# RMS norms of a hybrid decoder step: squares added on VectorE instead of by column-grouped products of ones

## Chip, cores and metric

One core of a Trainium2 chip runs the whole program. The metric is the device time of one execution in microseconds (us); the number quoted is the median of three runs.

## The reference

One inference step of a two-layer decoder. Layer 0 mixes tokens by gated DeltaNet (GDN), layer 1 by Mamba-2 SSD; each mixer is followed by a SwiGLU feed forward (FFN). Every sublayer stands between two RMS norms over the 1024 features of a token, and SSD has one more over its 2048 gated features:

```python
def rms_norm(x, w, eps=NORM_EPS):
    xf = x.astype(F32)
    return xf * lax.rsqrt(jnp.mean(xf * xf, axis=-1, keepdims=True) + eps) * w.astype(F32)
...
        hn = rms_norm(x, mix_pre_norm[i])
...
        x = x + rms_norm(out, mix_post_norm[i]).astype(x.dtype)
        hn = rms_norm(x, ffn_pre_norm[i])
        f = (jax.nn.silu(hn @ ffn_w_gate[i]) * (hn @ ffn_w_up[i])) @ ffn_w_down[i]
        x = x + rms_norm(f, ffn_post_norm[i]).astype(x.dtype)
...
    y = rms_norm(y * jax.nn.silu(z), norm_w)
```

There are 544 tokens: 512 of one prompt and 8 sampled sequences of 4. Everything is float32.

## The kernel before, in words

**Layout.** Activations lie feature-major: 128 features on the partitions, tokens along the free dimension. The 544 columns are worked as two halves A and B of `H2` = 272. The residual stream has 8 such tiles per half (`KD` = 8).

**Products.** `product` (L232) multiplies a weight tile with a half. Both operands are split in two exact parts, and three matmuls per 128x128 tile (L239, L240, L241: high by high, high by low, low by high) add up in PSUM. Weights come by DMA five pieces ahead (`AHEAD`, `fetch_to`); each 128x512 piece is split by ACT (`wh`, L211) and DVE (`wl`, L212).

**Norms.** `Pre` is the norm ahead of a sublayer, `Post` the one behind it, and `Post.finish` goes on into the next `Pre`, tile by tile. For each of 8 tiles of a half ACT writes the square (L414 from PSUM in `Post`, L374 from `x` in `Pre`). The sum over the features is made on TensorE: a matmul with `ones[:, 0:32]` as weights puts the column sums of one square on 32 partitions of the PSUM tile `ss`, four squares going to four groups of 32 partitions, and the second four on top of them (L427 in `Post.add`, four at a time; L379 in `Pre.sum`). DVE copies `ss` to SBUF (L435, L384). `rsq` then makes the sums token-major: four matmuls with 68 columns of `ss` as weights and the column `sel` as the moving operand (L346; for SSD's post norm also L348). `sel` holds 1/1024 on one partition of each group. `rsqrt` runs 11 Newton steps on DVE (L318 to L329, 68x4 elements, tiles `nx`, `ny`, `nh`, `nt`, `nu`). `spread` writes a diagonal `dg` (L335, DVE), and one more product of ones puts the factor `r` of each token on every partition (L338). `Post.finish` then does, for each of 8 tiles, `fw *= r` (L444, DVE), `x += fw` (L446, DVE, every third tile on GpSimd) and the square of `x`; ahead of an FFN also the split `xh` (L308, ACT) and `xl` (L309, DVE).

**SSD's own norm.** `gate` takes each of 16 tiles `ys` of 128x544: times the SiLU gate (L1535, DVE), squared on ACT. After each second tile four products of ones (L1547) put the column sums of two tiles by two halves on four groups of `yss`; DVE adds that to `ssacc` (copy L1551 the first time, L1553 seven times).

**Order.** An estimated clock (`Flow`) mixes the steps of norms and mixers, written as generators, with the stream of products when the program is recorded. Engines then run their own queues in that order. So that a norm has other work beside it, the last tiles of a sublayer run half A first (`ab`), and the next sublayer begins with a few tiles of half A alone (`start_first`; 4 pairs in FFN, `NL`; 3 tiles in SSD, `SLEAD`). A **transition** below is the stretch from the `dg` of the post norm of A to the `dg` of the next pre norm of B. There are three behind a sublayer (GDN to FFN, FFN to SSD, SSD to FFN); the last FFN has only the post norm.

Of the kernel before, what the change touches and what calls it, by code (L numbers as in the profile page):

```python
# [13 lines left out]
P = 128  # L14
D = 1024
KD = D // P            # feature tiles of the residual stream
SEQ = 512
NB = 8                 # sampled sequences
TS = 4                 # tokens of each
T = SEQ + NB * TS      # columns of every feature-major tile  # L20
H2 = T // 2            # columns of one product's moving operand
TQ = H2 // 4
NC = SEQ // P          # chunks of the prompt
KFF = 22
NSQ = 6                # squares that wait for their sums
AHEAD = 5              # weight pieces fetched ahead
NL = 4                 # feed forward's pairs that start before the second half's norm
NZ = 2                 # gates of SSD before its first x
ZLAG = 3               # x tiles of SSD before the next gate
SLEAD = 3              # SSD's tiles that start before the second half's norm  # L30
FINE = 12              # SSD's first products, with other work between their pieces
WIDE = 4               # SSD's first products, with more banks
NH0 = 4                # states of sampled sequences loaded ahead
PACE = 5.0             # between two updates of sampled states
LIVE = 3               # heads of GDN scanned side by side
# [3 lines left out]
# columns of the constant block  # L39
# [6 lines left out]
def constants():  # L46
# [8 lines left out]
    c[::32, C_SEL] = 1.0 / D  # L55
    c[0::64, C_SEL + 1] = 1e-6 / 2048
    c[32::64, C_SEL + 2] = 1e-6 / 2048
# [28 lines left out]
def _program(nc, tc, io, es):  # L86
# [23 lines left out]
    # ---------------------------------------------------------------- order of emission  # L110
    class Flow:
        """Interleaves generators with the stream of products, on an estimated clock (us).
        A generator yields (time on the tensor engine, time until its next step can start),
        or a condition that its next step waits for."""
# [73 lines left out]
    # ---------------------------------------------------------------- constants  # L188
# [13 lines left out]
    sely = [cst[:, C_SEL + 1 + i:C_SEL + 2 + i] for i in range(2)]  # L202
# [11 lines left out]
    # ---------------------------------------------------------------- weights  # L214
    # plan: the weight tiles in the order in which the products want them
# [83 lines left out]
    def stack(tile, src, first):  # L299
        """[96, n] of halves for one product of three: hi hi lo if first, else hi lo hi."""  # L300
# [31 lines left out]
    def spread(y):  # L332
        """[TQ, 4] with a token of a half on each element -> [P, H2], on every partition."""
# [7 lines left out]
    def rsq(ss, e, extra=None):  # L341
        """(mean + e) ** -0.5, token-major."""
        ps = bank("ms")[0:TQ, 0:4]
        for j in range(4):
            q = slice(TQ * j, TQ * j + TQ)
            PE.matmul(ps[:, j:j + 1], lhsT=ss[:, q], rhs=sel, start=True, stop=extra is None)  # L346
            if extra is not None:
                PE.matmul(ps[:, j:j + 1], lhsT=extra[1][:, q], rhs=extra[0], start=False, stop=True)  # L348
# [3 lines left out]


    class Pre:
        """st.x[hf] -> st.xh[hf], st.xl[hf]. free: without the norm's factor, which goes to
        st.r[hf] for the products' results."""

        def __init__(self, hf, kind, layer, free=False):
            self.hf, self.free, self.x = hf, free, st.x[hf]
            self.w = lambda k: nrm[:, kind, layer, k:k + 1]  # L360
            self.ps = bank("ss")
# [3 lines left out]

        def step(self, k):
            self.sum(k, self.square(k))

        def square(self, k):
# [3 lines left out]
            t = sqp.tile([P, H2], F32, tag="sq", name="sq", bufs=NSQ)  # L373
            S.activation(out=t, in_=x, func=AF.Square)  # L374
            return t

        def sum(self, k, t):
            g = k % 4
            PE.matmul(self.ps[32 * g:32 * g + 32, 0:H2], lhsT=ones[:, 0:32], rhs=t,  # L379
                      start=k < 4, stop=k >= KD - 4)  # L380

        def end(self):
            ss = sqp.tile([P, H2], F32, tag="ss", name="ss", bufs=1)
            V.tensor_copy(out=ss, in_=self.ps[:, 0:H2])  # L384
            y = rsq(ss, 1e-6)
# [17 lines left out]
    class Post:  # L403
        """Evacuates the tiles of a sublayer's last product, then post norm and residual."""

        def __init__(self, kind, layer, fw, e=1e-6, extra=None):
            self.kind, self.layer, self.fw, self.e, self.extra = kind, layer, fw, e, extra
            self.sq = [[], []]
            st.ready = [False, False]

        def tile(self, m):
            def done(hf, ps):
                t = sqp.tile([P, H2], F32, tag="sq", name="sq", bufs=NSQ)
                S.activation(out=t, in_=ps, func=AF.Square)  # L414
                S.activation(out=self.fw(m, hf), in_=ps, func=AF.Copy,
                             scale=nrm[:, self.kind, self.layer, m:m + 1])
                self.sq[hf].append(t)
                if len(self.sq[hf]) == 1:
                    self.ps = getattr(self, "ps", [None, None])
                    self.ps[hf] = bank("ss")  # L420
                if len(self.sq[hf]) % 4 == 0:
                    flow.start(self.add(hf, len(self.sq[hf]) - 4), 1.0)
            return done

        def add(self, hf, k0):
            for g in range(4):
                PE.matmul(self.ps[hf][32 * g:32 * g + 32, 0:H2], lhsT=ones[:, 0:32],  # L427
                          rhs=self.sq[hf][k0 + g], start=k0 == 0, stop=k0 == KD - 4)
            if k0 == KD - 4:
                yield 0.0, 0.5  # L430
                yield from self.finish(hf)

        def finish(self, hf):
            ss = sqp.tile([P, H2], F32, tag="ss", name="ss", bufs=1)
            V.tensor_copy(out=ss, in_=self.ps[hf][:, 0:H2])  # L435
            y = rsq(ss, self.e, None if self.extra is None else (sely[hf], self.extra))
# [4 lines left out]
            ts = []  # L441
            for k in range(KD):
# [4 lines left out]
                ts.append(pre.square(k))  # L447
                yield 0.1, 0.6
                if k % 4 == 3 and ts[k] is not None:
                    for j in range(k - 3, k + 1):  # L450
                        pre.sum(j, ts[j])
            yield from pre.end()

    def ab(tiles, operand, tail):
        """Both halves of each tile; the last ones A first, so that A's norm has company."""
# [1261 lines left out]
```

## Time and profile before

| | us |
|---|---|
| median of 3 runs (1797.18 to 1797.25) | 1797.25 |
| profiled execution: span | 1795.2 |
| time outside the span (median less span) | 2.05 |
| PE busy | 1746.4 (97%) |
| DVE busy | 1122.2 (63%) |
| ACT busy | 818.3 (46%) |
| POOL busy | 105.5 (6%) |
| mean granted TensorE clock | 0.981 of full speed |

The profile is of one execution. PE is TensorE's stream of matmuls, DVE is VectorE, ACT ScalarE, POOL GpSimd. One float32 matmul instruction leaves two records, so that "x6" of `ss` is three instructions. Records of the same kind that touch are merged in a timeline, and their number stands behind the x. A start and a duration are in us from the start of the span. A square bracket at the end of a row tells how long the engine had been idle before it, and who released it.

### The profile page before, as it was taken

How to read it: one execution, taken by the hardware profiler on the slowest of the kernel's cores; microseconds unless marked ns; L12 is line 12 of the kernel's file. 1: busy time of each engine (PE TensorE's matmuls, PEld its weight loads, DVE VectorE, ACT ScalarE, POOL GpSimd, SP SyncE). 2: the span in 40 equal slices, each digit the busy share in tenths (PEclk: the TensorE clock that was granted, in tenths of full speed). 3: DMA queues.
4: the chain of work that ended last, by engine and by line, in shares of the span. 5: the costliest groups of instructions: out<-in, count | busy, mean ns of one | idle time of the engine just before them, and what ended most of it. 6: DMA issues, size and time to landing. Idle time of an engine off the chain costs nothing. (4 is left out here: it accounts for less than half of the span.)

```text
span 1795.2 us, 37598 instructions
## 1 busy us (share of the span) xinstructions
PE 1746.4 (97%) x14447; PEld 1620.1 (90%) x14447; DVE 1122.2 (63%) x2966; ACT 818.3 (46%) x1824; POOL 105.5 (6%) x335
## 2 busy tenths in 40 slices
PE   6999999999999999999989999999999999999997
PEld 4888888898899999999787899999998999999996
DVE  5886856354876655323777886878348666664335
ACT  4765554345643333234555565657346433333242
POOL 0122112000000000000101110100000000000000
PEclk7999999799999999999999999999999999999998
DMA  5332323234354432234535544432434444444344
GB/s 140 103 93 79 91 71 107 77 109 137 114 182 140 141 112 83 77 92 141 175 105 155 166 131 140 133 103 64 141 129 147 159 147 141 142 140 139 122 130 124
DMA packets 163124, 220.89 MB, mean 123 GB/s; under 512 B 53184, under 2 KB 66048, under 8 KB 162432
## 3 DMA queue, kind: packets, MB, share of 16 engines
q1 hardware_dynamic: 162944, 218.49, 39.5%
q8 instruction: 113, 1.85, 0.4%
q14 instruction: 67, 0.55, 0.1%
HBM read 197.39 MB, written 21.04 MB: 122 GB/s over the span
## 5 line engine op out<-in xcount | busy, mean ns | idle before, releaser
L239 PE MATMUL mm<-xh,wh 128*128 128x272 f32 x2560 | 754.2, 295 | 3.2 <-ACT raw L534 2.3
L241 PE MATMUL mm<-xh,wl 128*128 128x272 f32 x2560 | 749.6, 293 | 1.9 <-issue 1.9
L240 PE MATMUL mm<-xl,wh 128*128 128x272 f32 x2560 | 746.8, 292 | 0.0
L212 DVE TENSOR_TENSOR wl<-wr,wh 128x512 fp32r<-128x512 f32 (+1 forms) x556 | 376.0, 679 | 328.6 <-ACT wh L211 316.8
L211 ACT ACTIVATE wh<-wr 128x512 fp32r<-128x512 f32 (+1 forms) x556 | 345.0, 622 | 446.7 <-PE mm L240 408.2
L239 PEld LDWEIGHTS mm<-xh,wh 128*128 128x128 f32 x2560 | 485.2, 190 | 24.3 <-issue 12.9
L241 PEld LDWEIGHTS mm<-xh,wl 128*128 128x128 f32 x2560 | 484.4, 189 | 8.9 <-issue 7.5
L240 PEld LDWEIGHTS mm<-xl,wh 128*128 128x128 f32 x2560 | 485.1, 190 | 6.7 <-issue 3.7
L239 PE MATMUL mm<-gb,wh 128*128 128x272 f32 x576 | 167.6, 292 | 0.0
L241 PE MATMUL mm<-gb,wl 128*128 128x272 f32 x576 | 165.1, 289 | 0.0
L240 PE MATMUL mm<-gb,wh 128*128 128x272 f32 x576 | 164.5, 288 | 0.0
L239 PEld LDWEIGHTS mm<-gb,wh 128*128 128x128 f32 x576 | 108.4, 188 | 5.4 <-issue 3.5
L547 DVE SCALAR_TENSOR_TENSOR conv<-raw,cw,conv 128x512 f32<-128x512 f32 x144 | 106.6, 741 | 8.4 <-ACT conv L544 7.9
L241 PEld LDWEIGHTS mm<-gb,wl 128*128 128x128 f32 x576 | 107.8, 188 | 1.2 <-issue 0.9
L240 PEld LDWEIGHTS mm<-gb,wh 128*128 128x128 f32 x576 | 107.9, 188 | 0.7 <-issue 0.4
L1172 ACT ACTIVATE sg<-sg 128x272 f32<-128x272 f32 x88 | 37.7, 431 | 99.7 <-DVE sg L1171 99.5
L446 POOL TENSOR_TENSOR x<-x,fw 128x272 f32<-128x272 f32 x16 | 14.8, 923 | 1087.0 <-DVE fw L444 658.9
L239 PE MATMUL mm<-yh,wh 128*128 128x272 f32 x256 | 75.1, 294 | 0.0
L240 PE MATMUL mm<-yl,wh 128*128 128x272 f32 x256 | 74.3, 290 | 0.4 <-DVE yl L309 0.4
L241 PE MATMUL mm<-yh,wl 128*128 128x272 f32 x256 | 73.9, 291 | 0.7 <-DVE wl L212 0.7
L211 ACT ACTIVATE gb<-sg 128x272 fp32r<-128x272 f32 x72 | 31.1, 432 | 93.6 <-DVE sg L1180 93.6
L1171 DVE TENSOR_TENSOR sg<-mm,r 128x272 f32<-128x272 f32 x88 | 38.6, 440 | 53.4 <-PE mm L241 51.7
(404 smaller groups left out, 2460.0 us busy)
## 6 DMA issues: line engine op xcount, KB each, us to landing
wr<-f_d_in SPq DMA_DIRECT2D x110, 256.0 KB
wr<-f_g_in SPq DMA_DIRECT2D x104, 256.0 KB
wr<-f_u_in SPq DMA_DIRECT2D x104, 256.0 KB
wr<-g_w_in SPq DMA_DIRECT2D x64, 256.0 KB
wr<-s_w_in SPq DMA_DIRECT2D x48, 256.0 KB
wr<-s_wo_in SPq DMA_DIRECT2D x44, 256.0 KB
wr<-s_wz_in SPq DMA_DIRECT2D x36, 256.0 KB
ar<-ad SPq DMA_DIRECT2D x32, 272.0 KB
```

The source lines that it names most:

```text
L211: S.activation(out=hi, in_=src, func=AF.Copy)
L212: V.tensor_tensor(out=lo, in0=src, in1=hi.bitcast(F32), op=ALU.subtract)
L239: PE.matmul(ps, lhsT=h[:, k, :], rhs=ah(k0 + k), start=first and k == 0, stop=False)
L240: PE.matmul(ps, lhsT=h[:, k, :], rhs=al(k0 + k), start=False, stop=False)
L241: PE.matmul(ps, lhsT=lo[:, k, :], rhs=ah(k0 + k), start=False, stop=last and k == n - 1)
L446: E.tensor_tensor(out=x[:, k, :], in0=x[:, k, :], in1=f, op=ALU.add)
L547: V.scalar_tensor_tensor(out=Y[:, 0:SEQ], in0=R[:, j:j + SEQ], scalar=w[:, j:j + 1], in1=Y[:, 0:SEQ], op0=ALU.mult, op1=ALU.add)
L1171: V.tensor_tensor(out=t, in0=ps, in1=st.r[hf], op=ALU.mult)
L1172: S.activation(out=t, in_=t, func=AF.Silu)
```

## The change

A class `Squares` keeps one tile `acc` of 128x272 in SBUF for each norm and half. The first square of a half is written by ACT straight into it; each later one goes to a tile `sq`, and DVE adds it to `acc` (`add`). The add of a square is issued only when the next square is issued, the last one in `sum`. The products into `ss`, and the copies of `ss`, are gone; the four token-major products take `acc` itself as weights, and `sel` is now 1/1024 on all 128 partitions. In SSD ACT writes the first gated square into `yacc` (128x544), and DVE adds 15 more. `Post.finish` starts 1.0 us after the eighth tile on the estimated clock, where it was 1.5 us. There are five `sq` tiles instead of six. (The diff of the whole file also strips comments, which is left out here.)

```diff
-NSQ = 6                # squares that wait for their sums
+NSQ = 5
...
-    c[::32, C_SEL] = 1.0 / D
-    c[0::64, C_SEL + 1] = 1e-6 / 2048
-    c[32::64, C_SEL + 2] = 1e-6 / 2048
+    c[:, C_SEL] = 1.0 / D
+    c[:, C_SEL + 1] = 1e-6 / 2048
...
-                PE.matmul(ps[:, j:j + 1], lhsT=extra[1][:, q], rhs=extra[0], start=False, stop=True)
+                PE.matmul(ps[:, j:j + 1], lhsT=extra[:, q], rhs=sely, start=False, stop=True)
...
+    class Squares:
+        def __init__(self):
+            self.acc = sqp.tile([P, H2], F32, tag="acc", name="acc", bufs=2)
+            self.n, self.late = 0, None
+
+        def square(self, src):
+            if self.n == 0:
+                S.activation(out=self.acc, in_=src, func=AF.Square)
+            else:
+                t = sqp.tile([P, H2], F32, tag="sq", name="sq", bufs=NSQ)
+                S.activation(out=t, in_=src, func=AF.Square)
+                self.add()
+                self.late = t
+            self.n += 1
+
+        def add(self):
+            if self.late is not None:
+                V.tensor_tensor(out=self.acc, in0=self.acc, in1=self.late, op=ALU.add)
+                self.late = None
+
+        def sum(self):
+            self.add()
+            return self.acc
...
     class Pre:
...
-            t = sqp.tile([P, H2], F32, tag="sq", name="sq", bufs=NSQ)
-            S.activation(out=t, in_=x, func=AF.Square)
-            return t
-
-        def sum(self, k, t):
-            g = k % 4
-            PE.matmul(self.ps[32 * g:32 * g + 32, 0:H2], lhsT=ones[:, 0:32], rhs=t,
-                      start=k < 4, stop=k >= KD - 4)
+            self.ss.square(x)
 
         def end(self):
-            ss = sqp.tile([P, H2], F32, tag="ss", name="ss", bufs=1)
-            V.tensor_copy(out=ss, in_=self.ps[:, 0:H2])
-            y = rsq(ss, 1e-6)
+            y = rsq(self.ss.sum(), 1e-6)
...
     class Post:
...
-                if len(self.sq[hf]) % 4 == 0:
-                    flow.start(self.add(hf, len(self.sq[hf]) - 4), 1.0)
+                if self.ss[hf].n == KD:
+                    flow.start(self.finish(hf), 1.0)
...
-        def add(self, hf, k0):
-            for g in range(4):
-                PE.matmul(self.ps[hf][32 * g:32 * g + 32, 0:H2], lhsT=ones[:, 0:32],
-                          rhs=self.sq[hf][k0 + g], start=k0 == 0, stop=k0 == KD - 4)
-            if k0 == KD - 4:
-                yield 0.0, 0.5
-                yield from self.finish(hf)
...
-            ss = sqp.tile([P, H2], F32, tag="ss", name="ss", bufs=1)
-            V.tensor_copy(out=ss, in_=self.ps[hf][:, 0:H2])
-            y = rsq(ss, self.e, None if self.extra is None else (sely[hf], self.extra))
+            y = rsq(self.ss[hf].sum(), self.e, None if self.extra is None else self.extra[:, half(hf)])
...
-                ts.append(pre.square(k))
-                yield 0.1, 0.6
-                if k % 4 == 3 and ts[k] is not None:
-                    for j in range(k - 3, k + 1):
-                        pre.sum(j, ts[j])
+                pre.square(k)
+                yield 0.0, 0.6
...
             S.activation(out=t, in_=y, func=AF.Square)
-            yield 0.0, 2.0
-            sqs.append(t)
...
-            ps = dbank("yss")
-            for j, t in enumerate((a, b)):
-                for h in range(2):
-                    r = 32 * (2 * j + h)
-                    PE.matmul(ps[r:r + 32, 0:H2], lhsT=ones[:, 0:32], rhs=t[:, half(h)],
-                              start=True, stop=True)
...
-                V.tensor_tensor(out=ssacc, in0=ssacc, in1=ps[:, 0:H2], op=ALU.add)
-            yield 0.6, 0.5
+            yield 0.0, 1.0
+            V.tensor_tensor(out=yacc, in0=yacc, in1=t, op=ALU.add)
```

Counted over the program, TensorE loses 160 matmul instructions (128 into `ss`, 32 into `yss`). DVE loses 24 (16 copies of `ss`, one copy and seven adds of `ssacc`) and gains 127 (112 adds of 128x272, 15 of 128x544). ACT, GpSimd and the DMA queues keep their counts.

TensorE's order in the GDN to FFN transition, at the end of GDN's last product (operands `oh`, `ol`) and the start of the FFN's first (`xh`, `xl`). Before:

```order
L241 MATMUL mm<-oh,wl 128x272
L427 MATMUL ss<-sq,cst 32x272 x3
L379 MATMUL ss<-sq,cst 32x272
L427 MATMUL ss<-sq,cst 32x272
L379 MATMUL ss<-sq,cst 32x272
L239 MATMUL mm<-xh,wh 128x272
L240 MATMUL mm<-xl,wh 128x272
```

With the change:

```order
L240 MATMUL mm<-oh,wl 128x272
L238 MATMUL mm<-xh,wh 128x272
L239 MATMUL mm<-xl,wh 128x272
L238 MATMUL mm<-xh,wh 128x272
L239 MATMUL mm<-xl,wh 128x272
L345 MATMUL ms<-cst,acc 68x1 x4
```

The products of ones between the two sublayers are gone, and the token-major products come after two tiles of the next one.

DVE's order in the same transition, while half B goes through `Post.finish` and half A's first FFN tiles are evacuated (`sg`). Before:

```order
L1171 TENSOR_TENSOR sg<-mm,r 128x272
L444 TENSOR_TENSOR fw<-fw,r 128x272
L212 TENSOR_TENSOR wl<-wr,wh 128x512
L1174 TENSOR_TENSOR sg<-sg,r 128x272
L446 TENSOR_TENSOR x<-x,fw 128x272
L212 TENSOR_TENSOR wl<-wr,wh 128x512
L1180 TENSOR_TENSOR sg<-sg,mm 128x272
L309 SCALAR_TENSOR_TENSOR xl<-x,nrm,xh 128x272
L444 TENSOR_TENSOR fw<-fw,r 128x272
```

With the change:

```order
L1168 TENSOR_TENSOR sg<-mm,r 128x272
L444 TENSOR_TENSOR fw<-fw,r 128x272
L373 TENSOR_TENSOR acc<-acc,sq 128x272
L1171 TENSOR_TENSOR sg<-sg,r 128x272
L446 TENSOR_TENSOR x<-x,fw 128x272
L211 TENSOR_TENSOR wl<-wr,wh 128x512 x2
L308 SCALAR_TENSOR_TENSOR xl<-x,nrm,xh 128x272
L1177 TENSOR_TENSOR sg<-sg,mm 128x272
L444 TENSOR_TENSOR fw<-fw,r 128x272
L373 TENSOR_TENSOR acc<-acc,sq 128x272
```

Each tile of the norm brings one add more into the queue, in front of the evacuations and weight splits behind it.

DVE's order in the FFN to SSD transition, half B behind its post norm's `dg`. Before:

```order
L444 TENSOR_TENSOR fw<-fw,r 128x272 x2
L446 TENSOR_TENSOR x<-x,fw 128x272 x2
L444 TENSOR_TENSOR fw<-fw,r 128x272 x3
L446 TENSOR_TENSOR x<-x,fw 128x272 x2
L444 TENSOR_TENSOR fw<-fw,r 128x272 x3
L446 TENSOR_TENSOR x<-x,fw 128x272 x2
L384 COPY ss<-ss 128x272
L318 TENSOR_SCALAR nx<-ms 68x4
```

With the change:

```order
L444 TENSOR_TENSOR fw<-fw,r 128x272
L373 TENSOR_TENSOR acc<-acc,sq 128x272
L446 TENSOR_TENSOR x<-x,fw 128x272
L444 TENSOR_TENSOR fw<-fw,r 128x272 x2
L446 TENSOR_TENSOR x<-x,fw 128x272
L373 TENSOR_TENSOR acc<-acc,sq 128x272
L444 TENSOR_TENSOR fw<-fw,r 128x272
L373 TENSOR_TENSOR acc<-acc,sq 128x272
L446 TENSOR_TENSOR x<-x,fw 128x272
L373 TENSOR_TENSOR acc<-acc,sq 128x272
```

The adds stand between the `fw` and `x` of one chain, and the copy of `ss` at its end is replaced by the last of them.

## Rows read from the trace of the kernel before

**Rows 1.** The page, part 1: busy time, share of span, instructions.
```profile
PE 1746.4 (97%) x14447; PEld 1620.1 (90%) x14447; DVE 1122.2 (63%) x2966; ACT 818.3 (46%) x1824; POOL 105.5 (6%) x335
```
**Rows 2.** Waits of PE: who for whom: us in total, times, longest.
```profile
PE r L338 <- DVE dg L335: 14.8, 7, 6.8
```
**Rows 3.** Busy time by stretch away from the transitions; columns as headed.
```profile
core 0: us, PE busy (x) PEld busy (x) DVE busy (x) ACT busy (x) POOL busy (x), PEclk, DMA share, GB/s
417.00:437.00 20.00, 20.00 (x151) 16.97 (x150) 6.67 (x10) 10.22 (x22) 0.00 (x0) 1.00 0.38 120
795.00:850.00 55.00, 55.00 (x432) 51.86 (x431) 20.00 (x32) 23.05 (x45) 0.00 (x0) 1.00 0.43 127
1040.00:1240.00 200.00, 200.00 (x1664) 185.27 (x1664) 153.77 (x413) 114.55 (x244) 19.59 (x61) 1.00 0.38 119
...
1700.00:1756.00 56.00, 56.00 (x439) 52.75 (x438) 20.95 (x36) 23.14 (x45) 0.00 (x0) 1.00 0.44 129
```
**Rows 4.** Tile `ss`, sublayers' last products: records, ns min/median/max, first to last.
```profile
L427 PE MATMUL ss<-sq,cst x24: 392/405/417, 417.7 to 437.3; 128*32 128x272 f32 x24
...
L427 PE MATMUL ss<-sq,cst x24: 392/405/417, 1701.3 to 1755.3; 128*32 128x272 f32 x24
```
**Rows 5.** Timeline of PE, SSD's last product: start, duration, instruction.
```profile
1332.07 0.29 PE L241 MATMUL mm<-yh,wl 128*128 128x272 f32 x1
1332.29 0.66 PE L427 MATMUL ss<-sq,cst 128*32 128x272 f32 x6
...
1333.11 0.29 PE L240 MATMUL mm<-yl,wh 128*128 128x272 f32 x1
1333.23 0.29 PE L241 MATMUL mm<-yh,wl 128*128 128x272 f32 x1
1333.45 0.65 PE L427 MATMUL ss<-sq,cst 128*32 128x272 f32 x2
...
1334.26 0.29 PE L240 MATMUL mm<-yl,wh 128*128 128x272 f32 x1
```
**Rows 6.** Busy time by stretch, PE on tile `yss` alone, all of SSD.
```profile
960.00:1260.00 300.00, 7.83 (x64) 1.00 0.39 125
```
**Rows 7.** Busy time in the three transitions; columns as in rows 3.
```profile
442.48:496.70 54.22, 52.98 (x382) 44.52 (x381) 44.61 (x125) 32.93 (x73) 3.70 (x4) 1.00 0.36 117
854.81:901.06 46.25, 40.19 (x285) 31.98 (x284) 35.83 (x104) 25.22 (x55) 4.88 (x13) 0.96 0.59 189
1339.41:1399.70 60.29, 59.81 (x446) 51.95 (x445) 50.91 (x130) 36.23 (x78) 3.92 (x4) 1.00 0.44 142
```
**Rows 8.** Timeline of DVE, GDN to FFN.
```profile
473.26 0.43 DVE L1171 TENSOR_TENSOR sg<-mm,r 128x272 f32<-128x272 f32 x1
473.61 0.42 DVE L444 TENSOR_TENSOR fw<-fw,r 128x272 f32<-128x272 f32 x1
```
**Rows 9.** Timeline of DVE, GDN to FFN: its longest waits.
```profile
457.94 0.16 DVE L318 TENSOR_SCALAR nx<-ms 68x4 f32<-68x4 f32 x1 [2.46 <-PE ms L346]
...
489.41 0.44 DVE L384 COPY ss<-ss 128x272 f32<-128x272 f32 x1 [2.83 <-PE ss L379]
```
**Rows 10.** Timelines of POOL and of DVE, GDN to FFN, half A.
```profile
445.77 0.77 POOL L446 TENSOR_TENSOR x<-x,fw 128x272 f32<-128x272 f32 x1 [111.52 <-DVE fw L444]
...
445.83 1.02 DVE L309 SCALAR_TENSOR_TENSOR xl<-x,nrm,xh 128x272 fp32r<-128x272 f32 x1 [0.19 <-ACT xh L308]
...
447.12 0.49 DVE L309 SCALAR_TENSOR_TENSOR xl<-x,nrm,xh 128x272 fp32r<-128x272 f32 x1
```
**Rows 11.** Timeline of PE, FFN to SSD, half B.
```profile
893.04 1.33 PE L379 MATMUL ss<-sq,cst 128*32 128x272 f32 x4 [1.93 <-ACT sq L374]
...
901.64 1.25 PE L338 MATMUL r<-dg,cst 68*128 68x272 f32 x2 [2.56 <-DVE dg L335]
```
**Rows 12.** The last post norm: timeline of ACT, and chain of waits.
```profile
1780.59 0.40 ACT L414 ACTIVATE sq<-mm 128x272 f32<-128x272 f32 x1 [5.41 <-PE mm L241]
...
1780.56 1.15 PE ss L427 x8
...
1782.22 0.67 PE ms L346 x8
```

More of the change, by code (lines that the diff above doesn't have):

```diff
@@ L201, in _program @@
     sel = cst[:, C_SEL:C_SEL + 1]
-    sely = [cst[:, C_SEL + 1 + i:C_SEL + 2 + i] for i in range(2)]
+    sely = cst[:, C_SEL + 1:C_SEL + 2]
     I4 = cst[:, C_I4:C_I4 + 32]
@@ L360, in __init__ @@
             self.w = lambda k: nrm[:, kind, layer, k:k + 1]
-            self.ps = bank("ss")
+            self.ss = Squares()
             self.xh = act.tile([P, KD, H2], F32R, tag="x", name="xh")
@@ L364, in __init__ @@
             st.xh[hf], st.xl[hf] = self.xh, self.xl
-        def step(self, k):
-            self.sum(k, self.square(k))
         def square(self, k):
@@ L407, in __init__ @@
             self.kind, self.layer, self.fw, self.e, self.extra = kind, layer, fw, e, extra
-            self.sq = [[], []]
+            self.ss = [None, None]
             st.ready = [False, False]
@@ L412, in done @@
             def done(hf, ps):
-                t = sqp.tile([P, H2], F32, tag="sq", name="sq", bufs=NSQ)
-                S.activation(out=t, in_=ps, func=AF.Square)
+                if self.ss[hf] is None:
+                    self.ss[hf] = Squares()
+                self.ss[hf].square(ps)
                 S.activation(out=self.fw(m, hf), in_=ps, func=AF.Copy,
                              scale=nrm[:, self.kind, self.layer, m:m + 1])
[L417 to L420, printed above, removed]
-                if len(self.sq[hf]) % 4 == 0:
-                    flow.start(self.add(hf, len(self.sq[hf]) - 4), 1.0)
-            return done
-        def add(self, hf, k0):
-            for g in range(4):
-                PE.matmul(self.ps[hf][32 * g:32 * g + 32, 0:H2], lhsT=ones[:, 0:32],
-                          rhs=self.sq[hf][k0 + g], start=k0 == 0, stop=k0 == KD - 4)
-            if k0 == KD - 4:
-                yield 0.0, 0.5
-                yield from self.finish(hf)
+                if self.ss[hf].n == KD:
+                    flow.start(self.finish(hf), 1.0)
+            return done
         def finish(self, hf):
-            ss = sqp.tile([P, H2], F32, tag="ss", name="ss", bufs=1)
-            V.tensor_copy(out=ss, in_=self.ps[hf][:, 0:H2])
-            y = rsq(ss, self.e, None if self.extra is None else (sely[hf], self.extra))
+            y = rsq(self.ss[hf].sum(), self.e, None if self.extra is None else self.extra[:, half(hf)])
             yield 0.0, 1.0
@@ L440, in finish @@
             pre = self.pre(hf)
-            ts = []
             for k in range(KD):
@@ L469, in _program @@
         for k in range(KD):
-            pre.step(k)
+            pre.square(k)
     for pre in pres:
@@ L1261, in ssd @@
         dma(sdt, io["s_dt"].partition_broadcast(P))
-        ssacc = one.tile([P, H2], F32, name="ssacc")
+        yacc = one.tile([P, T], F32, name="yacc")
         cm = cone.tile([P, NB * 36], F32, name="cm")
@@ L1517, in x_task @@
             d.done = True
-        sz, sqs = {}, []
+        sz = {}
         def z_done(m):
@@ L1535, in gate @@
             V.tensor_tensor(out=y, in0=y, in1=t, op=ALU.mult)
-            S.activation(out=t, in_=y, func=AF.Square)
-            yield 0.0, 2.0
-            sqs.append(t)
-            if len(sqs) < 2:
-                return
-            a, b = sqs
-            sqs.clear()
-            ps = dbank("yss")
-            for j, t in enumerate((a, b)):
-                for h in range(2):
-                    r = 32 * (2 * j + h)
-                    PE.matmul(ps[r:r + 32, 0:H2], lhsT=ones[:, 0:32], rhs=t[:, half(h)],
-                              start=True, stop=True)
             if not hasattr(st, "first"):
                 st.first = True
-                V.tensor_copy(out=ssacc, in_=ps[:, 0:H2])
-            else:
-                V.tensor_tensor(out=ssacc, in0=ssacc, in1=ps[:, 0:H2], op=ALU.add)
-            yield 0.6, 0.5
+                S.activation(out=yacc, in_=y, func=AF.Square)
+                return
+            S.activation(out=t, in_=y, func=AF.Square)
+            yield 0.0, 1.0
+            V.tensor_tensor(out=yacc, in0=yacc, in1=t, op=ALU.add)
         W = io["s_w"]
@@ L1608, in ssd @@
         fw = [t544("fw") for _ in range(KD)]
-        post = Post(1, 1, lambda m, hf: fw[m][:, half(hf)], 1e-12, ssacc)
+        post = Post(1, 1, lambda m, hf: fw[m][:, half(hf)], 1e-12, yacc)
         post.pre = lambda hf: Pre(hf, 2, 1, True)
```

## The prediction

> **What bounds the kernel now.** I begin with the page's busy times. PE is busy for 97% of the span, DVE for 63% [rows 1]. A kernel like that gets faster where PE has less to do, unless another engine then paces it. So the second question goes to the stretches. In four steady stretches, in which a sublayer's last product runs, and in SSD, PE is busy all the time at the full granted clock, while DVE works 20.00 of 55 us there, or 6.67 of 20, and 153.77 of 200 in SSD [rows 3]. There PE alone sets the pace. In the three transitions PE is busy for 52.98 of 54.22 us, 40.19 of 46.25 and 59.81 of 60.29, but DVE for 44.61, 35.83 and 50.91 [rows 7]: PE is first, DVE a close second. The list of waits says what PE lacks when it lacks something: 14.8 us in seven waits for `dg`, the last step of a norm on DVE [rows 2].
>
> **The price of a visit.** A timeline shows what a product of ones costs in a stream of weight products. One product matmul follows another every 0.127 us (55.00 us over 432 records, [rows 3]). Around three `ss` instructions (six records) the start of L241 at 1332.07 and that of L240 at 1333.11 lie 1.04 us apart where two steps, 0.25, would do: the visit costs 0.79. The next visit has one instruction and costs 1.03 - 0.25 = 0.78 [rows 5]. So the price is for the interruption, not for the number of products. If it were only the length of a record, 0.39 us at the least [rows 4], a visit would be worth half of that.
>
> The Trainium skill ("TensorE: Matmul & The Clock Gate", Part 3, Measured speedup vs the span model) has a rule that speaks against this change: products in different column groups run side by side, about 4 ns apart, so that four cost hardly more than one. The trace agrees that three cost as much as one, but at twice the length of the record. By the rule alone a visit is worth some 0.40 us, an estimate, and the steady term below would be 8.8 and not 17.2 us.
>
> **The change part by part.** The sum is made against the profiled span, 1795.2 us; 2.05 us lie outside it up to the median, 1797.25, and I take them as unchanged.
>
> *Steady stretches.* The last products of the four sublayers contain 24 `ss` records each (two per instruction) [rows 4], which the timeline shows in 6, 5, 6 and 5 visits. They go: 22 x 0.78 = **17.2 us**. The adds that replace them (7 per half, 0.35 us of issue each: `sg` at 473.26 and `fw` at 473.61, [rows 8]) lie beside products, with DVE busy about 36% there [rows 3]; without that cover they would cost 56 x 0.35 = 20 us.
>
> *SSD.* PE spends 7.83 us in `yss` [rows 6], in twelve visits; some are next to state products that interrupt the stream anyway, so I take the busy time, **7.8 us**, and not 12 x 0.78 = 9.4; at the least half, 4. DVE gets 15 adds of 128x544, at twice the 272-column step 0.7 each, 10.5 us, and loses eight small ones, 2.8. With 46 of 200 us free [rows 3] that is covered.
>
> *Start and end.* At the start only the norms run; I credit **0.5 us**, between 0 and one visit, 0.78. At the end the chain goes from 1780.56 (the `ss` products) to 1782.22 (`ms`). Now the last square, which starts at 1780.59 and takes 0.40, is followed by one add of 0.43 [rows 8], so `ms` can start near 1781.5: **0.7 us** [rows 12].
>
> *Transitions.* Here PE loses 12, 6 and 11 visits, but DVE gains 17 adds and loses three copies in each: 17 x 0.35 - 3 x 0.36 = 4.9 us. In GDN to FFN DVE's work becomes 44.61 + 4.9 = 49.5 us, while PE's falls to 52.98 - 12 x 0.78 = 43.6 [rows 7]. DVE now paces. It still has to wait at the ends of the chains, 2.46 us for `ms` and 2.83 for the last squares' sum [rows 9]; with the copy's round trip gone I leave 3 us of waits, so 52.5 against 54.22: **1.7 us**. In SSD to FFN the order puts 22 product matmuls more ahead of B's factor, 2.8 us of work that stood behind it, with some 0.7 us of splits. DVE needs 50.91 + 4.9 + 0.7 + 3 = 59.5, against 60.29 + 2.8 = 63.1: **3.6 us**. FFN to SSD is a chain in which PE waits for squares (1.93) and for `dg` (2.56) [rows 11]. Its first part loses six visits, 4.7 us; in its second the adds between `fw` and `x` lengthen DVE's chain by up to 8 x 0.35 = 2.8, less the copy and half a visit. I take **1.5 us**, about midway between 4.7 - 1.8 = 2.9 and nothing. If no wait of DVE stayed, the three would give 4.7, 4.9 (46.25 less 35.83 + 4.9 + 0.6 of splits) and 6.6, together 16.2; if all of DVE's present idle time stayed, they would lose 4.9 and 4.9 and 2.8, together 12.6.
>
> *Small things.* Five `sq` tiles for six cost nothing while each add follows its square by one tile. The counts of ACT, POOL and DMA instructions stay.
>
> Sum: 17.2 + 7.8 + 0.5 + 0.7 + 1.7 + 3.6 + 1.5 = 33.0 us. The span becomes 1762.2, and the time **1764 us**.
>
> **The rivals.** *PE paces the transitions too.* If the scheduler's order lets DVE's adds slip into its idle time, the visits' full price comes back: 29 x 0.78 = 22.6 instead of 6.8, in all 48.8, so 1748; with 16.2, 1755. For it: DVE has 9.6, 10.4 and 9.4 us idle. Against it: that idle time is waiting inside the norm's chain, which the adds lengthen.
>
> *DVE's idle time stays, and more.* Each add stands in a chain of `fw`, `x`, square and add, over DVE and ACT, and DVE's queue is in order, so an add whose square is not ready holds the evacuations behind it. With all idle time kept, the gain is 26.2 - 12.6 = 13.6, so 1784; with half of that loss, 1777. DVE is also held by GpSimd: `xl` takes 1.02 us beside POOL's `x` and 0.49 without [rows 10]. Twelve such `x` stand in loops that get adds, so up to 12 x 0.53 = 6.4 us, 1770. The Trainium skill ("SBUF — State Buffer", SBUF: two separate sides) has this as a lock: a DVE operation with two SBUF inputs and a GpSimd operation that reads SBUF exclude each other. The adds have two SBUF inputs, as `xl` has, and the rows agree.
>
> *The steady stretches do not pay.* If weights, not PE, set their pace, PE would wait for `wl` instead, and only the transitions, start and end count: 1789. Against it: PE is busy 100% there, DMA 0.38 to 0.44 [rows 3].
>
> *Slower.* The adds of `Post` and of SSD are queued ahead of weight splits. If an add stood waiting for ACT's square of the tile just finished, then `wl` would come late and PE would stop once for each of 56 + 15 adds, for 0.40 + 0.43 = 0.83 us [rows 8, 12]: 59 us lost against 33 gained, 1797 + 26 = 1823. It decides from 33 / 71 = 0.46 us per add. Against it: the add of a square is issued only with the next square, a whole product of at least 24 x 0.127 = 3 us later, and weights are fetched five pieces ahead.
>
> *It doesn't do what it says.* The order shows the `ss` and `yss` products gone, so I give that nothing.
>
> **How the numbers follow.** My forecast, DVE pacing the transitions with some waits left, gets 0.53, with a range of its own from 1756 to 1771. PE pacing everything, 1746 to 1756, gets 0.22. DVE's idle time kept or its queue held, 1771 to 1784, gets 0.18, in it 0.01 for a visit worth no more than its record: 22 x 0.39 = 8.6 us less gain, 1772, against which the rows show 0.78. Steady stretches without pay get 0.04, slower 0.03. The range from 1748 to 1780 leaves out a small part of the second case (0.04), of the third (0.04) and the last two (0.07), some 0.15. A measurement here tells a difference from about 0.2%, 3.6 us. All cases but the last lie further below 1797.25 than that; a thin remainder where gains and losses meet gets 0.03 for no change, slower 0.03, faster 0.94.
>
> **What would show it.** Right: no `ss` or `yss` records, PE busy 45 to 50 us less, the steady stretches 3.9 to 4.7 us shorter each with PE still at 100%, SSD some 8 us shorter; adds of 0.43 us on DVE, whose busy time grows by about 48 us (112 x 0.43 + 15 x 0.71 less 24 x 0.44); in the two transitions to FFN DVE busy for over 90% and PE with new waits for `dg` beyond 14.8 us in all. Wrong: PE waits for `wl` in steady stretches or in SSD (the last two rivals); PE still at 98% in the transitions and the time near 1750 (the first); transitions longer than before (the second).

## The result and the profile after

The changed kernel took 1768.7 us (median of 4 runs, 1765.33 to 1778.71) beside 1797.22 us for the kernel before (4 runs, 1784.13 to 1797.25). The ratio is 0.9891, with a 95% interval of 0.9854 to 0.9927: faster, by about 1.1%. (It is not the quotient of the two medians, 0.9841: 0.9891 is 1768.7 over 1788.24, the median of the 15 runs of the kernel before that stand beside e1.) The forecast was 1764 us, a ratio of 0.9815 to 1797.25.

Executions of either kernel differ by some 13 us. Much of this lies in the GDN mixer, which the change does not touch: it took 355.3 to 368.4 us in the thirteen profiles of this study, by how long TensorE's granted clock lies at the lower of its two levels there. Its mean over the mixer was 0.94 in the kernel before (368.0 us), 0.96 in the changed one (362.9) and 0.99 in e4 (355.4). The windows of 50 us that hold such a stretch show it, first in the kernel before, then in the changed one:

```profile
100.00:150.00 50.00, 47.07 (x621) 41.51 (x620) 41.56 (x140) 30.25 (x79) 11.86 (x37) 1.00 0.31 74
300.00:350.00 50.00, 48.61 (x553) 39.75 (x553) 18.26 (x52) 16.43 (x49) 4.05 (x16) 0.76 0.27 83
```

```profile
100.00:150.00 50.00, 48.56 (x590) 41.89 (x589) 37.97 (x133) 28.04 (x71) 10.93 (x37) 0.86 0.30 79
300.00:350.00 50.00, 49.15 (x637) 41.29 (x637) 25.85 (x70) 21.25 (x62) 6.99 (x20) 1.00 0.34 98
```

PEclk (third column from the end) was 0.76 in one and 0.86 in the other, at different places. So below I compare two executions stretch by stretch and leave the GDN mixer out. The boundaries are the starts of the `dg` on DVE, of which there are 20 in each trace. The third column is a second profiled execution of the same changed kernel (experiment e5), the fourth the best kernel of the study (e1).

| stretch, us | before | changed | changed, e5 | adds in post norms and SSD only, e1 |
|---|---|---|---|---|
| start, to the second `dg` | 22.9 | 25.5 | 24.2 | 23.5 |
| GDN mixer, to the first of its own `dg` | 368.0 | 362.9 | 356.1 | 359.0 |
| GDN's last product, to post norm A | 43.3 | 39.4 | 39.4 | 39.1 |
| transition GDN to FFN | 54.2 | 56.1 | 53.0 | 54.1 |
| first FFN, to post norm A | 358.1 | 354.4 | 352.6 | 351.9 |
| transition FFN to SSD | 46.3 | 49.9 | 48.4 | 45.3 |
| SSD, mixer | 370.6 | 367.8 | 366.9 | 365.4 |
| SSD, last product, to post norm A | 67.8 | 63.4 | 63.4 | 63.4 |
| transition SSD to FFN | 60.3 | 60.9 | 62.3 | 61.3 |
| second FFN, to post norm A | 361.2 | 353.4 | 353.2 | 355.2 |
| end | 34.3 | 35.0 | 35.2 | 34.7 |
| whole span | 1795.2 | 1776.9 | 1763.0 | 1761.3 |
| span less the GDN mixer | 1427.2 | 1414.0 | 1406.9 | 1402.3 |

(The GDN mixer has four `dg` of its own ahead of its last product; the 8.3 us between them are in no row and the same in all. SSD is divided at ACT's 357th split of a weight piece, which lies in its last product, behind the last product into `yss` and ahead of the first into `ss`.) Outside the GDN mixer the change is thus worth 13 to 20 us where 33 were forecast; the kernel before was profiled once. The steady stretches give what they should. FFN to SSD and SSD to FFN lengthen where they should have shortened, and GDN to FFN does so in one execution of two.

The page's first part of the changed kernel, as [rows 1]:

```profile
PE 1697.0 (96%) x14127; PEld 1612.5 (91%) x14127; DVE 1162.0 (65%) x3069; ACT 818.0 (46%) x1824; POOL 110.2 (6%) x335
```

PE is busy 49 us less, DVE 40 us more. The steady stretches, as [rows 3], are still PE's alone, with DVE at 37 to 43% of them and 82% in SSD:

```profile
405.00:425.00 20.00, 20.00 (x161) 20.00 (x160) 8.62 (x16) 10.21 (x23) 0.00 (x0) 1.00 0.47 149
790.00:830.00 40.00, 40.00 (x317) 39.63 (x316) 14.71 (x26) 15.90 (x31) 0.00 (x0) 1.00 0.41 116
1016.00:1216.00 200.00, 200.00 (x1652) 187.43 (x1652) 163.79 (x440) 117.78 (x248) 22.76 (x67) 1.00 0.42 126
...
1690.00:1735.00 45.00, 45.00 (x360) 44.86 (x359) 18.79 (x31) 19.37 (x37) 0.00 (x0) 1.00 0.50 143
```

The transitions, as [rows 7], have changed places: DVE is now busy for 49.13 of 56.12 us, 42.43 of 49.86 and 53.68 of 60.89, and PE stands still for 8, 15 and 6 us of them (before 1, 6 and less than 1).

```profile
436.08:492.20 56.12, 48.29 (x327) 46.70 (x326) 49.13 (x138) 32.02 (x72) 3.49 (x4) 0.85 0.36 116
846.59:896.45 49.86, 34.79 (x258) 33.10 (x256) 42.43 (x120) 25.58 (x56) 4.99 (x13) 0.87 0.56 174
1327.59:1388.48 60.89, 54.82 (x424) 52.11 (x423) 53.68 (x145) 36.84 (x79) 5.58 (x4) 1.00 0.45 140
```

The list of PE's waits names the new one, beside the old of [rows 2]:

```profile
PE ms L345 <- DVE acc L373: 31.0, 6, 12.0
PE r L337 <- DVE dg L334: 13.9, 5, 6.4
PE mm L240 <- DVE wl L211: 5.1, 8, 1.3
```

The token-major products `ms` read `acc`, and wait for the last add; 14.9 of the 31.0 us, the longest wait of 12.0 among them, lie at the start, where there is nothing else to do. The waits for `wl`, 0.7 us in all before, lie in the transitions, 3.7 of the 5.1 us in SSD to FFN, but for one of 0.8 us in SSD that was there before; none is in a steady stretch. What the wait for `acc` brings with it stands in the timeline of PE in GDN to FFN and in windows of 4 us from there on:

```profile
444.19 0.29 PE L239 MATMUL mm<-xl,wh 128*128 128x272 f32 x1
449.10 1.06 PE L345 MATMUL ms<-cst,acc 128*68 128x1 f32 x8 [4.62 <-DVE acc L373]
...
450.62 0.43 PE L239 MATMUL mm<-xl,wh 128*128 128x272 f32 x1
450.85 0.43 PE L240 MATMUL mm<-xh,wl 128*128 128x272 f32 x1
```

```profile
444.00:448.00 4.00, 0.48 (x4) 0.26 (x2) 4.00 (x11) 3.64 (x11) 0.76 (x1) 0.82 0.00 0
448.00:452.00 4.00, 2.90 (x21) 2.90 (x21) 3.38 (x11) 0.84 (x2) 0.00 (x0) 0.50 0.22 66
452.00:456.00 4.00, 4.00 (x19) 4.00 (x19) 3.88 (x21) 1.26 (x2) 0.00 (x0) 0.50 0.61 178
456.00:460.00 4.00, 4.00 (x28) 3.92 (x28) 2.20 (x9) 1.89 (x4) 0.00 (x0) 0.90 0.50 154
```

The four matmuls ahead of `ms` are two pairs of `xh,wh` and `xl,wh`; the third matmul of a step, `xh,wl`, comes only behind it. Between them PE runs nothing for 4.62 us, while DVE is busy all the time. `ms` is not the only one that waits. The FFN's first `wl` stands in DVE's queue right behind the add that releases `ms`, 12.9 us behind the `dg`; in the kernel before it came 10.0 us behind it:

```profile
448.61 0.43 DVE L373 TENSOR_TENSOR acc<-acc,sq 128x272 f32<-128x272 f32 x1
448.97 0.68 DVE L211 TENSOR_TENSOR wl<-wr,wh 128x512 fp32r<-128x512 f32 x1
```

```profile
452.51 1.28 DVE L212 TENSOR_TENSOR wl<-wr,wh 128x512 fp32r<-128x512 f32 x2
```

In e4, where DVE wrote that first `wl` ahead of the norm's work, PE stopped a little further on, for the second one:

```profile
443.84 0.59 PE L243 MATMUL mm<-xh,wl 128*128 128x272 f32 x1 [5.25 <-DVE wl L214]
```

So DVE's queue holds PE here, by whichever of its results is wanted first. After the pause the granted clock is 0.50, the lower level (1.2 GHz), and product matmuls come 0.23 us apart in place of 0.126, until about 456 us.

This pause did not decide the length of the transition. The second execution, e5, has it too, 4.62 us with a clock of 0.50 behind it, and took 53.0 us from `dg` to `dg`, less than the kernel before (54.2) and than e1 (54.1). The 56.1 us of the first hold another stop, of 2.27 us at 482.73 for a `wh` whose weights came late (ACT had waited 2.97 us for the transfer); e5 has none there.

In FFN to SSD the pause is 9.56 us:

```profile
883.57 0.29 PE L240 MATMUL mm<-xh,wl 128*128 128x272 f32 x1
893.42 1.04 PE L345 MATMUL ms<-cst,acc 128*68 128x1 f32 x8 [9.56 <-DVE acc L373]
```

Here the lead tiles of half A are done, 3.5 us behind B's `dg`, where they lasted to 0.6 us ahead of it before; behind `ms` stand the factor `r` of half B and what follows it. What got longer is half B's chain on DVE, from `dg` to `dg`: 16.1 us, and 15.9 in e5, where it was 11.2 before (12.1 in e7, which leaves it as it was). It holds seven adds, and four weight splits `wl` where two stood before.

### The profile page after: what moved, and what is told of

The parts are those of the page before. It is cut to its first block, busy times and chain, and to the rows that moved or that the text cites. A ratio compares the mean times of both kernels' runs of the same rounds, so it can differ in the third digit from the quotient of the medians.

```text
span 1776.9 us, 37092 instructions
## 1 busy us (share of the span) xinstructions
PE 1697.0 (96%) x14127; PEld 1612.5 (91%) x14127; DVE 1162.0 (65%) x3069; ACT 818.0 (46%) x1824; POOL 110.2 (6%) x335
## 4 chain that ended last, share of the span: by engine, by line
PE 88%; DVE 6%; ACT 2%; DMA 2%; issue 1%; POOL 0%; SPq 0%; DVEq 0%; ACTq 0%; POOLq 0%
PE mm L238 25%; PE mm L240 25%; PE mm L239 24%; DVE acc L373 1%; PE yd L1495 1%; PE yos L1386 1%; PE yo L1500 1%; PE su L1472 1%; DVE wl L211 1%; PE mm L247 1%; DVE fw L444 1%; PE r L337 1%; PE sc L985 1%; PE ms L345 1%; PE su L573 1%
## 5 line engine op out<-in xcount | busy, mean ns | idle before, releaser
L373 DVE TENSOR_TENSOR acc<-acc,sq 128x272 f32<-128x272 f32 x112 | 50.1, 448 | 45.9 <-ACT sq L366 45.3
```

The lines of the kernel that those rows point to most:

```text
L373: V.tensor_tensor(out=self.acc, in0=self.acc, in1=self.late, op=ALU.add)
```

## The experiments

Theory A: the adds of the pre norms, 14 of the 17 in each transition, lie in the chain that DVE paces there and give away what the visits return. Rival B: not the adds but the new order costs, since `Post.finish` starts half a microsecond earlier and cuts in elsewhere. Rival C: GpSimd and VectorE hold each other up. Figures "outside the GDN mixer" are the profiled span less that stretch, as in the table; those of the changed kernel are 1414.0 and 1406.9 us.

**e1, adds in the post norms and SSD only.** The pre norms go back to products of ones, on the changed kernel:

```diff
 class Pre:
-            self.ss = Squares()
+            self.ps = bank("ss")
...
-            self.ss.square(x)
+            t = sqp.tile([P, H2], F32, tag="sq", name="sq", bufs=NSQ)
+            S.activation(out=t, in_=x, func=AF.Square)
+            return t
+        def sum(self, k, t):
+            g = k % 4
+            PE.matmul(self.ps[32 * g:32 * g + 32, 0:H2], lhsT=ones[:, 0:32], rhs=t,
+                      start=k < 4, stop=k >= KD - 4)
```

> The adds on VectorE are kept in the post norms and in SSD's gated norm; the pre norms sum their squares on TensorE again, as before the change. Compared by stretch, since the granted clock inside the GDN mixer differs from run to run. Theory A (the adds of the pre norms, 14 of the 17 in each transition, lie in the chain that VectorE paces there, and give away what the visits return): the three transitions are back near those of the kernel before, 54, 46 and 60 us (plus or minus 2), and the steady stretches and SSD keep the shortening that the changed kernel has there, 4.4, 2.7, 6.2, 3.6 and 4.8 us, so some 5 us less than the changed kernel at equal clock. Rival B (the order: the post norm's chain now starts half a microsecond earlier on the estimated clock and cuts in elsewhere; the adds themselves are free): GDN to FFN and FFN to SSD stay at 56 and 50 us or so, and the time stays within 2 us of the changed kernel's.

Measured: 1762.79 us (4 runs, 1761.88 to 1763.06) beside 1788.24 for the kernel before (15 runs), ratio 0.9853 (0.983 to 0.9876). The transitions are back:

```profile
429.92:484.03 54.11, 53.83 (x381) 45.23 (x380) 46.82 (x129) 33.66 (x76) 4.03 (x4) 1.00 0.40 124
835.94:881.24 45.30, 40.00 (x290) 33.39 (x288) 37.05 (x108) 25.80 (x56) 4.68 (x13) 0.93 0.63 197
1310.07:1371.40 61.33, 60.77 (x444) 52.59 (x443) 51.29 (x134) 36.31 (x79) 3.24 (x4) 1.00 0.45 142
```

PE is busy throughout the first and third again, and the clock is 1.00 in them. The rest of the gain stayed. Outside the GDN mixer it is 5 to 12 us under the changed kernel. `Post.finish` starts early here too, so rival B is out as the main cause. Something of it is there: in FFN to SSD half B's chain has the four weight splits here too, and takes 13.3 us (12.4 in e6) without any add, beside 11.2 before.

**e2, adds in the pre norms only.** The same edit the other way round: `Post` and SSD as before the change, `Pre` with `Squares`.

> Only the pre norms add on VectorE; the post norms and SSD sum on TensorE as before the change. Theory A: steady stretches and SSD as before (within 1 us each); the transitions are longer than before by 0 to 4 us each, the start by 1 to 2, and the whole is 3 to 10 us slower than before at equal clock although some 23 visits of 0.78 us are gone from the transitions. Rival B: the transitions are as before or up to 6 us shorter each, and the whole is faster than before.

Measured: 1794.97 us (10 runs) beside 1788.24, ratio 1.0038 (1.0019 to 1.0057): slower. Transitions 55.3, 48.6 and 62.0 us, the start 24.9; outside the GDN mixer 1430.8 beside 1427.2. The pre norms' visits are gone from PE, and nothing came of it, as A says. Half B's chain in FFN to SSD takes 13.5 us, with the adds but only two weight splits.

**e3, the pre norms' adds doubled.** In the changed kernel:

```diff
         def add(self):
             t = self.late.pop(0)
+            for _ in range(self.dose):          # 1 in Pre, 0 in Post
+                self.eng.tensor_tensor(out=t, in0=t, in1=t, op=ALU.max)
             self.eng.tensor_tensor(out=self.acc, in0=self.acc, in1=t, op=ALU.add)
```

> The changed kernel with each add of the pre norms preceded by one operation more on VectorE of the same size (the square's maximum with itself, which leaves it as it is): 42 more in the transitions, 14 at the start. Theory A (VectorE paces the transitions): each costs its 0.35 us there, so some 4 to 5 us more in each transition and 2 to 4 at the start, 14 to 19 us in all. Rival B (adds are free in the transitions, the order costs): under 4 us in all.

Measured: 1797.37 us (6 runs), ratio 1.0048 (1.0021 to 1.0075), so all of the gain is lost. The start is 28.8, the transitions 59.7, 53.4 and 66.2: against the two executions of the changed kernel 3.3 to 4.6 us longer at the start and 3.6 to 6.7, 3.5 to 5.0 and 3.9 to 5.3 in the transitions. For 14 operations each that is 0.25 to 0.5 us apiece: in a transition little hides DVE's work. Outside the GDN mixer the time is 1428.8 us, 15 to 22 more than the changed kernel's; 14 to 19 were expected.

**e4, the post norms' adds doubled.** The same line in `Post`'s `Squares`.

> The changed kernel with each add of the post norms preceded by one operation more of the same size: 56 more, most of them in the steady stretches, some 3 of each sublayer behind the first dg of a transition. Theory A: nothing in the steady stretches (under 0.5 us each), at most 1 us in each transition and 0.4 at the end, 0 to 4 us in all. If the steady adds held VectorE's queue in front of the weight splits (the slower rival of the prediction), 0.3 us or more for each, 15 us and more.

Measured: 1774.62 us (4 runs), ratio 0.992 (0.9896 to 0.9943). The steady stretches are 40.4 (from 39.4), 352.8 (352.6 to 354.4), 63.8 (63.4) and 353.7 (353.3); GDN to FFN grew to 58.7, the others did not, and the end is 35.5. Some 45 more operations beside products cost at most about 2 us: the cover is real, and the slower rival of the prediction is out. GDN to FFN, with the stop of 5.25 us shown above, took more than the 1 us that I allowed, and GDN's last product 1.0 where I allowed 0.5.

**e5, the changed kernel again, and e6, e1 again**, on one chip.

> The changed kernel once more, with more runs, beside the kernel before and the next three on one chip. By the stretches of the two profiles the change is worth about 18 us at equal granted clock in the GDN mixer (forecast 33): 1765 to 1779, as far as the clock there allows.

> The kernel of the first experiment once more (adds in the post norms and SSD only). Theory A: under the changed kernel by what the transitions and the start cost there, 5 to 8 us, in runs of one chip, and so the fastest of before, changed and this. Rival B: equal to the changed kernel within 2 us, and the 1763 of the first look was the clock's luck.

Measured: 1772.84 (6 runs, 1764.82 to 1778.97) and 1766.72 (6 runs, 1764.37 to 1776.36), beside 1787.91 (18 runs). The ratios are 0.9903 (0.987 to 0.9935) and 0.9879 (0.9848 to 0.991); these intervals overlap. The stretches decide: 1406.9 us outside the GDN mixer for e5 and 1402.9 for e6, transitions 54.1, 44.5 and 61.5 in e6. So e1's kernel is the fastest of the three, by 4 to 12 us in the profiles; the medians say the same with less certainty. Its lead of 4 to 5 us on e5's profile comes from FFN to SSD above all (3 to 4 us); in GDN to FFN it is 1.1 us behind.

**e7, adds in SSD's gated norm only.**

> Only SSD's gated norm adds on VectorE; post and pre norms sum on TensorE as before. The forecast charged 7.8 us for its 32 products. If a visit next to a state product costs less than its own busy time, since the stream is interrupted there anyway, the stretch from SSD's first norm to the first piece of its last product is 5 us shorter, not 8; every other stretch is as before within 1 us.

Measured: 1786.78 us (10 runs), ratio 0.9984 (0.9959 to 1.0008), no clear difference. SSD, from its first norm to its post norm, is 436.4 beside 438.3, so 1.9 us shorter where 5 were expected, though the first transition moved by 0.8 and the second by 0.9 the other way without any edit there. In the changed kernel, e1 and e6 the mixer's part is 2.8, 5.1 and 3.5 us shorter than before. I take 2 to 5 us for this term; the reason for the difference from 7.8, that these visits often stand beside state products, was argued from the order alone.

**e8, adds in half A's pre norms, products in half B's.**

> As the first experiment, but the pre norms of half A (three of them, not the one at the start) add on VectorE too, while those of half B stay on TensorE. In the changed kernel half A's part of GDN to FFN was 0.8 us shorter than before and half B's 3.6 us longer. If what the adds cost comes from the evacuations that share VectorE with half B's chain, GDN to FFN falls to about 52 us and FFN to SSD stays at 45, and the time is 1 to 4 us under the first experiment's. If any add in a transition costs its 0.25 us or more, the transitions are 1 to 3 us longer than there.

Measured: 1766.92 us (5 runs), ratio 0.9896 (0.9858 to 0.9935); transitions 53.0, 46.9 and 61.8, outside the GDN mixer 1406.0. GDN to FFN is 1 us shorter than in e1, FFN to SSD 1.6 longer. No gain over e1: that half A's adds are free came true in GDN to FFN alone.

**e9 and e10, the price of a visit.** The changed kernel with one, and with four, products of ones put back at 42 places whose sums nobody reads:

```diff
                 self.ss[hf].square(ps)
+                if not self.last and self.ss[hf].n > 1:
+                    ps = bank("ss")
+                    for g in range(1):          # e10: range(4)
+                        PE.matmul(ps[32 * g:32 * g + 32, 0:H2], lhsT=ones[:, 0:32],
+                                  rhs=self.ss[hf].late[0], start=True, stop=True)
```

> The changed kernel with 42 products of ones put back, one after each square but the first of a half in the post norms of GDN, of the first FFN and of SSD; nobody reads their result. If the price is the interruption, about 0.78 us each: 33 us in all, in GDN's last product about 9 visits or 7 us up to the first dg, the same in the others. If it is the length of a record, 0.39 us: 16 us in all.

> The same with four products at each of the 42 places, in four column groups, so 168. If a visit costs the same for four as for one, this is within 2 us of the run with one (42 times 0.01 to 0.02). If each product costs, it is 100 us more (126 times 0.78) or 49 (126 times 0.39).

Measured: 1789.81 and 1792.38 us (9 runs each), ratios 0.9995 (0.9976 to 1.0013) and 1.0015 (0.999 to 1.004): the whole gain is gone, and four cost hardly more than one. A visit in GDN's last product, in the timeline of PE, with one instruction and then with four:

```profile
402.16 0.29 PE L243 MATMUL mm<-oh,wl 128*128 128x272 f32 x1
402.39 0.65 PE L443 MATMUL ss<-sq,cst 128*32 128x272 f32 x2
402.96 0.39 PE L241 MATMUL mm<-oh,wh 128*128 128x272 f32 x1
403.20 0.29 PE L242 MATMUL mm<-ol,wh 128*128 128x272 f32 x1
```

```profile
394.95 0.29 PE L243 MATMUL mm<-oh,wl 128*128 128x272 f32 x1
395.18 0.67 PE L443 MATMUL ss<-sq,cst 128*32 128x272 f32 x8
395.78 0.39 PE L241 MATMUL mm<-oh,wh 128*128 128x272 f32 x1
396.01 0.29 PE L242 MATMUL mm<-ol,wh 128*128 128x272 f32 x1
```

From the matmul ahead to the second behind it are 1.04 and 1.06 us, where two steps of 0.126 would do: 0.79 and 0.81 a visit, and the other visits between two product matmuls there cost 0.82 to 0.86. GDN's last product, with ten of them, grew by 6.8 and 7.0 us.

The whole cost less than the 33 us expected for 42 visits: outside the GDN mixer e9 takes 1430.3 us, 16 to 23 more than the changed kernel. The 32 visits in the last products lengthen each of these by some 7 us. The other ten stand in the transitions, which take 54.1, 49.8 and 60.7 us, no more than in the changed kernel: where PE waits for DVE, a visit costs nothing that shows.

**e11, the pre norms' adds on GpSimd**: `G.tensor_tensor` for `V.tensor_tensor` in `Pre`'s `Squares`.

> The changed kernel with the adds of the pre norms on GpSimd (0.92 us each by the residual adds there) instead of VectorE. If VectorE and GpSimd work undisturbed side by side, the 14 adds of a transition leave VectorE's queue and the transitions come to those of the first experiment, 54, 45 and 61 us, plus a GpSimd add of 0.9 in place of 0.4 at the end of each chain. If they exclude each other on operations with two inputs in SBUF, many operations of VectorE beside the 42 adds take up to 1.0 us in place of 0.43 to 0.49, and the transitions are no shorter than the changed kernel's, 53 to 56, 48 to 50, 61 to 62, or up to 4 us longer each; the start, where 14 such adds stand in a row, is 5 us or more longer.

Measured: 1781.81 us (10 runs), ratio 0.9944 (0.9925 to 0.9963), and outside the GDN mixer 1418.8 us, 5 to 12 more than the changed kernel. Start 27.3, transitions 58.4, 50.1 and 62.0. In the rows of tile `acc` the adds take 0.84 us on GpSimd, and a DVE add up to 1.05:

```profile
L377 POOL TENSOR_TENSOR acc<-acc,sq x56: 755/837/1203, 6.6 to 1379.5; 128x272 f32<-128x272 f32 x56
L377 DVE TENSOR_TENSOR acc<-acc,sq x56: 427/435/1047, 398.8 to 1761.1; 128x272 f32<-128x272 f32 x56
```

Beside GpSimd's adds and `x`, 30 operations of DVE on 128x272 tiles took more than 0.6 us, 15 us more in sum than at 0.45 each; in the changed kernel ten did, 3.7 us. So rival C is a real mechanism, but small in the change itself, and no way out of it. The kernel before has eight such operations, also 3.7 us, so the change brought no more of this than was there. How much of e11's longer transitions is this, and how much the slower chain of adds, these runs do not separate. The start, 27.3, grew by 2 to 3 us where 5 or more were expected.

## Why the prediction was right or wrong

The time fell inside the range, and faster was right. But outside the GDN mixer the gain is 13 to 20 us, not 33, and that 1768.7 lies so near to 1764 is in part luck: the forecast took too large a gain from too high a start. It went out from three runs at 1797.2; the medians of 15, 18 and 25 later runs of the same kernel are 1788.24, 1787.91 and 1789.9, and 33 us less would be 1755 to 1757. Beside the first two of these medians the changed kernel gains 20 us (1768.7) and 15 us (e5). By the steps:

- **The price of a visit** was right where PE sets the pace. It is paid per interruption; e9 and e10 show it directly, 0.79 for one instruction and 0.81 for four. In the transitions e9's visits cost nothing that shows.
- **Steady stretches, 17.2 us.** Right. GDN's, the first FFN's and SSD's last products are 3.9, 3.7 to 5.5 and 4.4 us shorter, the second FFN's 7.8 to 7.9, in which lie the 2.8 us of products that moved ahead of B's factor. Together 17 to 19 us without those. The adds beside them cost nothing that could be seen; e4 doubled them for at most about 2 us.
- **The end, 0.7 us.** Right: from the start of the last product matmul to the end 14.93 us before, 14.11 and 14.31 after.
- **The start, 0.5 us gained.** Wrong in sign, 1.3 to 2.6 us lost. The second half's adds stand between the Newton steps of the first on DVE. Part is the arrival of `x`: e1, with products there, also needed 23.5 and e6 23.0, against 22.9.
- **SSD, 7.8 us.** Mis-sized; it measured 2 to 5.
- **Transitions, 6.8 us gained.** This is the step that failed: "DVE now paces ... I leave 3 us of waits", and for FFN to SSD "I take 1.5 us". Together they took 2.9 and 6.1 us longer (53.0 + 48.4 + 62.3 and 56.1 + 49.9 + 60.9 against 160.8), of which 2.8 are the products moved into the third. DVE's work was forecast well: 49.5 us in GDN to FFN, measured 49.13 and 49.23; 41.3 in FFN to SSD, measured 42.43 and 42.27. What failed is the time that DVE stands still: 7.0, 7.4 and 7.2 us, in e5 3.8, 6.1 and 8.6, where the sum left 3 in the two transitions to an FFN. So GDN to FFN came out as forecast in e5 (53.0 beside 52.5) and 3.6 us longer in the other execution; SSD to FFN took 60.9 and 62.3 where 59.5 were set. In FFN to SSD the first part, up to B's `dg`, gained 1.3 and 2.5 us of the 4.7 for its visits, and the second lost 4.9 and 4.7 where 1.8 was set: the adds lie in that chain, and two more weight splits as well, which this term did not have. By e1 and e6, which have the splits and not the adds, the adds are 2.6 to 3.7 us of it. I added up DVE's work and did not price the order in its queue, in which both the chain and the `wl` that PE wants stand behind the adds.
- **Signs.** PE's busy time fell by 49 us, as said. DVE's grew by 40, not 48: the 48 adds up durations of 0.43, though one operation follows another after 0.35. The new waits of PE are for `acc`, not for `dg`, whose sum hardly changed (13.9 us). A slip in the second rival, without effect on its time: with the 0.6 us of splits counted in the case without waits, all of DVE's idle time kept loses 5.5 us in FFN to SSD and not 4.9.
- **The rivals.** "DVE's idle time stays, and more" (0.18) is nearest to what happened: 1784 at its worst, 1777 at half. By the gain outside the GDN mixer, 1797 less 13 to 20, the time is 1777 to 1784. "PE paces the transitions too", priced 1748, did not come true with the adds; e1, in which PE does pace them, takes 25 us off outside the GDN mixer without removing their visits.
- **The hold beside GpSimd**, up to 6.4 us, came to little: three of the 112 adds took 0.67 to 1.02 us in place of 0.43, 1.4 us more in all. One of them, in the timelines of POOL and DVE:

```profile
888.47 0.82 POOL L446 TENSOR_TENSOR x<-x,fw 128x272 f32<-128x272 f32 x1 [2.44 <-DVE fw L444]
...
888.60 1.00 DVE L373 TENSOR_TENSOR acc<-acc,sq 128x272 f32<-128x272 f32 x1
```

  By the lock that the Trainium skill describes ("SBUF — State Buffer", SBUF: two separate sides) such a pair excludes each other; this row and e11 agree.

## What to carry to other kernels

Count what a side product costs where it interrupts the stream, not by its own record: here 0.8 us for one or four alike, and next to nothing where the stream waits anyway. Moving such work to another engine pays where that engine idles (the steady stretches), and takes it back where the same engine already carries the chain that everyone waits for (the transitions); so move it place by place, as e1 does. And where another engine is to set the pace, do not only add up its work: look at which of its results is wanted next, and at what stands ahead of that result in its queue.

## What the runs showed that I had not expected

Products run slowly after a pause of PE. In GDN to FFN 4.62 us of waiting for DVE were followed by a granted clock of 0.50 from 448 to 456 us, with products at 0.23 us in place of 0.126; the same place in e5 shows the same pause and clock, and e1, without the pause, had 1.00 throughout that transition. What this costs the program is not shown: e5's transition is 1.1 us shorter than e1's all the same.

One profile of each kernel does not tell the size of such a change. The mixer that no experiment touched took 355.3 to 368.4 us, and outside it two executions of the changed kernel differ by 7 us, 1414.0 and 1406.9.
